# Ten attention weights of a hybrid decoder layer: their two parts made on GpSimd instead of ScalarE and VectorE

## The chip, the cores and the metric

The kernel runs on one core of a Trainium2 chip. A core has five engines that run side by side, each with its own queue of instructions: TensorE (PE, matrix products; its weight loads appear as PEld), VectorE (DVE), ScalarE (ACT), GpSimd (POOL) and SyncE (SP, which here issues DMAs). They pass data through SBUF and, for TensorE's results, PSUM. The metric is device time in microseconds (us) for one execution; less is better.

## The reference

One inference step of one layer on a prompt of 4096 tokens and 8 single-token samples, model width 1024, fp32:

- RMSNorm, then one projection by `w_in` into RG-LRU input (512), RG-LRU gate (512), queries (512), keys (128), values (128) and attention gate (512).
- Recurrence: a causal convolution of width 4, two block-diagonal gates r and i, h_t = a_t h_(t-1) + sqrt(1 - a_t^2) (i_t x_t) with a_t = sigmoid(L)^(8 r_t), times SiLU of its gate.
- Attention: 8 query heads on 2 key heads of 64, a sliding window of 128 keys, a relative-position bias, a sink per head, softmax; times SiLU of its gate.
- Both groups side by side, output projection by `w_out`, RMSNorm, residual. The states of convolution, recurrence and key/value window are outputs too.

## The kernel before

The 4096 tokens go in chunks: the first of 256 tokens with the 8 samples (264 columns), then ten of 384. Part A runs over all chunks: it normalizes and transposes x, projects it for the recurrence (`pr`), convolves, makes the gates (`gt`) and scans (line 352). It leaves the transposed x and its results in DRAM (`xT_d`, `mix_d`, line 362). Part B runs over all chunks again for attention: value, key, query and gate projections (`pv`, `pk`, `pq`, `pga`), then units of scores `S`, softmax, transposed probabilities `pT` and their product with the values `po`. Part C is the output projection.

Every fp32 product is split into three: a weight `ws` is turned into a rounded part `wh` and a rest `wl = ws - wh`, x into `xh` and `xl`, and `mm3` sums wh.xh + wh.xl + wl.xh. A projection of 128 output columns is thus 8 x 3 products. `load_w` makes the parts: the DMA to the staging tile `ws` (line 105, two buffers), the cast to `wh` by ACT (line 111), and the subtraction for `wl` by the engine `eng` (line 112), DVE unless told otherwise. Part A's first two weights already have their subtraction on GpSimd, after a cast on DVE (line 109).

The ten weights of part B are loaded in one loop (lines 754 to 757), in the order V, Q0, K, Q1, Q2, Q3, G0, G1, G2, G3 (G is the attention gate). The first eight take the eight slots of part A's weights, each as soon as part A's last product with the old weight is done; the last two lie in a pool `pb_late`, whose memory belongs to part A's last steps until these end. The loads of x for part B are issued by SP too (line 499).

The order of the instructions on each engine is not that of the code: a scheduler simulates the program with costs of its own and sets each engine's order when the kernel is built. An engine then works through its queue strictly in that order, and an instruction whose input or buffer isn't ready holds up all behind it. PE's projections in part B alternate between two PSUM banks: the products of Q2 can start when ACT and DVE have read K's bank, those of G0 when the copies and subtractions that make `sq` of Q2 (lines 567 to 570) have read Q2's.

The lines that matter around the hand-over from A to B: `thr`, `thi` (333, 334), `tt` (337), `aa`, `uu` (340, 341), the square root `uu` on ACT (348), the multiplications (350) and scans (352) of part A's last chunk; `kt` (487, 489), `ksT` (534), `sq` (567 to 570), masks (622), the minima `nm` (625), `ph` and `pl` (642, 643) of part B's first chunk.

Of the kernel before, what the change touches and what calls it, by code (L numbers as in the profile page):

```python
# [44 lines left out]
def hymba_kernel(ctx: ExitStack, tc: tile.TileContext, ins, outs):  # L45
    nc = tc.nc
# [56 lines left out]
    def load_w(src, n, pool, bufs=None, spare=None, eng=nc.vector, fast=False):  # L103
        ws = (spare or stage).tile([P, KD, P], F32, tag="ws", name=f"ws_{n}")
        nc.sync.dma_start(ws, src)
        wh = pool.tile([P, KD, P], F32R, tag="wh", name=f"wh_{n}", bufs=bufs)
        wl = pool.tile([P, KD, P], F32R, tag="wl", name=f"wl_{n}", bufs=bufs)
        if fast:
            nc.vector.tensor_copy(wh, ws)
        else:  # L110
            act(wh, ws, AF.Copy)
        eng.tensor_sub(wl, ws, wh)
        return wh, wl

    def load_w_in(m, pool=None, bufs=None, spare=None, eng=nc.vector, fast=False):
        return load_w(w_in_v[:, :, m * P:(m + 1) * P], f"in{m}", pool or wpool, bufs, spare, eng, fast)

    def load_w_out(e):
        return load_w(w_out_v[:, e, :].rearrange("p (k c) -> p k c", c=P), f"out{e}", wpool)
# [296 lines left out]
    wB = {}  # L416
# [335 lines left out]
    pbl, pb, pb1 = [c.__enter__() for c in cms]  # L752
    xB = load_x(0)
    for item in B_FIRST:
        if item[0] in "KVQG":
            m = {"K": 12, "V": 13, "Q": 8, "G": 14}[item[0]] + (int(item[1]) if item[0] in "QG" else 0)
            wB[m] = load_w_in(m) if len(wB) < 8 else load_w_in(m, pbl, 2)
    state = [{} for _ in chunks]
    state[0]["xs"] = xB
    work = [chunk_B(ci, state[ci], state[ci - 1]) for ci in range(NCH)]  # L760
# [121 lines left out]
def build(nc, arrays):  # L882
    args = []
    for name in _INS + ['onehot']:
        a = arrays[f"in_{name}_dram"]
        args.append(nc.dram_tensor(f"in_{name}_dram", a.shape, mybir.dt.from_np(a.dtype), kind="ExternalInput").ap())
    res = []
    for i, (shape, dtype) in enumerate(_OUTS):
        res.append(nc.dram_tensor(f"out_{i}_dram", shape, F32, kind="ExternalOutput").ap())
    with tile.TileContext(nc, schedule_with_timeline_sim=True) as tc:  # L890
        hymba_kernel(tc, args, res)
# [13 lines left out]
```

## Time and profile before

| | us |
|---|---|
| median of 3 runs | 1445.58 (1444.28 to 1446.62) |
| the profiled execution | 1449.84 |
| its span, first to last instruction | 1448.1 |
| PE busy | 1403.7 (97%) |
| DVE busy | 915.0 (63%) |
| ACT busy | 799.9 (55%) |
| POOL busy | 440.8 (30%) |

The profile is of one execution. Busy time counts an engine's own instructions; PE at 97% says that over the whole span there are some 44 us in which it had nothing to do. The tables by stretches say where those are, and the granted clock (1.00 is the full 2.4 GHz) how fast PE was allowed to run there. A wait row names the instruction that waited and the one on another engine that released it.

### The profile page before, as it was taken

What the parts mean: (1) busy time and instruction counts of PE and PEld (TensorE: products, weight loads), DVE (VectorE), ACT (ScalarE), POOL (GpSimd) and SP (SyncE); (2) the same over time, 40 slices, a digit from 0 to 9 for tenths busy, and PEclk for the clock granted to TensorE, in tenths of its full rate; (3) what the DMA queues carried; (4) which work ended last, traced back from release to release, by engine and by line L of the source; (5) the groups of instructions that cost most, each with busy time, mean ns of one, the idle gap of its engine ahead of it and who ended that gap; (6) DMA issues with size and microseconds to landing.
All of it is one profiled execution on the core that took longest, in us unless ns stands there. A gap on an engine that the chain in (4) does not pass through costs nothing.

```text
span 1448.1 us, 24120 instructions
## 1 busy us (share of the span) xinstructions
PE 1403.7 (97%) x8127; PEld 1324.1 (91%) x8127; DVE 915.0 (63%) x2258; ACT 799.9 (55%) x2055; POOL 440.8 (30%) x876
## 2 busy tenths in 40 slices
PE   5999999999999889999999999999999999999998
PEld 4999989999999789999999999999998888888886
DVE  6778877777778767657566566566784445334433
ACT  4656656755655656567676676576783222222211
POOL 3233332222421023364463453453543000000000
PEclk9999999999999989999999999999999999999999
DMA  8324454433236330320320320330444534443431
GB/s 269 134 85 153 148 169 143 148 136 129 98 127 192 99 117 25 122 100 13 109 99 12 110 99 12 110 99 12 162 134 148 165 136 141 146 132 133 147 128 60
DMA packets 115028, 170.23 MB, mean 118 GB/s; under 512 B 12214, under 2 KB 98822, under 8 KB 114906
## 3 DMA queue, kind: packets, MB, share of 16 engines
q1 hardware_dynamic: 114906, 168.71, 34.8%
q8 instruction: 64, 1.05, 0.3%
q14 instruction: 58, 0.48, 0.1%
HBM read 100.19 MB, written 68.50 MB: 116 GB/s over the span
## 4 chain that ended last, share of the span: by engine, by line
PE 68%; DVE 3%; ACT 2%; DMA 1%; issue 1%; SPq 0%; POOLq 0%; DVEq 0%; ACTq 0%
PE out L822 8%; PE out L824 8%; PE out L823 8%; PE pga L122 4%; PE pga L123 4%; PE pga L124 4%; PE pq L123 4%; PE pq L122 4%; PE pq L124 4%; PE po L664 3%; PE pT L638 2%; PE S L604 2%; PE S L605 2%; PE pr L122 1%; PE pr L123 1%; PE pr L124 1%
## 5 line engine op out<-in xcount | busy, mean ns | idle before, releaser
L123 PE MATMUL pr<-xl,wh_in 128*128 128x384 f32 (+1 forms) x688 | 231.9, 338 | 0.0
L122 PE MATMUL pr<-xh,wh_in 128*128 128x384 f32 (+1 forms) x688 | 220.1, 340 | 10.1 <-ACT xc L302 10.1
L124 PE MATMUL pr<-xh,wl_in 128*128 128x384 f32 (+1 forms) x688 | 229.8, 336 | 0.0
L822 PE MATMUL out<-wh_out,xh_mix_d 128*128 128x512 f32 (+1 forms) x520 | 201.2, 387 | 0.0
L823 PE MATMUL out<-wl_out,xh_mix_d 128*128 128x512 f32 (+1 forms) x520 | 200.9, 386 | 0.0
L824 PE MATMUL out<-wh_out,xl_mix_d 128*128 128x512 f32 (+1 forms) x520 | 200.5, 386 | 0.0
L841 ACT ACTIVATE sqc<-out 128x512 bf16<-128x512 f32 (+2 forms) x67 | 39.2, 585 | 192.5 <-PE out L824 182.4
L122 PEld LDWEIGHTS pr<-xh,wh_in 128*128 128x128 f32 x688 | 129.9, 191 | 11.9 <-ACT xc L302 11.6
L630 ACT ACTIVATE tt<-tt,nm 128x129 f32<-128x129 f32 x256 | 100.0, 393 | 71.9 <-DVE nm L627 71.7
L844 DVE TENSOR_TENSOR out<-out,gpost 128x512 f32<-128x512 f32 (+1 forms) x65 | 45.4, 699 | 148.0 <-ACT sqc L841 147.3
L123 PEld LDWEIGHTS pr<-xl,wh_in 128*128 128x128 f32 x688 | 131.3, 191 | 0.7 <-issue 0.7
L124 PEld LDWEIGHTS pr<-xh,wl_in 128*128 128x128 f32 x688 | 131.3, 191 | 0.0
L123 PE MATMUL pga<-xl_B,wh_in 128*128 128x384 f32 (+1 forms) x352 | 119.7, 340 | 0.0
L122 PE MATMUL pga<-xh_B,wh_in 128*128 128x384 f32 (+1 forms) x352 | 118.9, 338 | 0.7 <-ACT qz L574 0.7
L122 PE MATMUL pq<-xh_B,wh_in 128*128 128x384 f32 (+1 forms) x352 | 117.0, 333 | 1.3 <-DVE ksT L534 0.7
L124 PE MATMUL pga<-xh_B,wl_in 128*128 128x384 f32 (+1 forms) x352 | 118.0, 335 | 0.0
L123 PE MATMUL pq<-xl_B,wh_in 128*128 128x384 f32 (+1 forms) x352 | 117.3, 333 | 0.0
L124 PE MATMUL pq<-xh_B,wl_in 128*128 128x384 f32 (+1 forms) x352 | 117.1, 333 | 0.0
L141 POOL TENSOR_TENSOR rs_c<-ssc,mhalf 128x1 f32<-128x1 f32 (+1 forms) x33 | 20.5, 622 | 314.9 <-DVE ssc L845 286.2
L822 PEld LDWEIGHTS out<-wh_out,xh_mix_d 128*128 128x128 f32 x520 | 97.7, 188 | 19.9 <-issue 0.2
L824 PEld LDWEIGHTS out<-wh_out,xl_mix_d 128*128 128x128 f32 x520 | 97.7, 188 | 19.7
L823 PEld LDWEIGHTS out<-wl_out,xh_mix_d 128*128 128x128 f32 x520 | 97.7, 188 | 19.3
(258 smaller groups left out, 3565.0 us busy)
## 6 DMA issues: line engine op xcount, KB each, us to landing
xs<-in_x_prompt_dram SPq DMA_DIRECT2D x32, 512.0 KB
xr<-in_x_prompt_dram SPq DMA_DIRECT2D x32, 512.0 KB
out_dram<-xr SPq DMA_DIRECT2D x31, 512.0 KB
xT_d<-xh SPq DMA_DIRECT2D x80, 192.0 KB
xT_d<-xl SPq DMA_DIRECT2D x80, 192.0 KB
xf_mix_d<-mix_d SPq DMA_DIRECT2D x80, 192.0 KB
xh_B<-xT_d SPq DMA_DIRECT2D x80, 192.0 KB
xl_B<-xT_d SPq DMA_DIRECT2D x80, 192.0 KB
```

The costliest lines, as they stand in the source:

```text
L122: nc.tensor.matmul(out, wh, xh, start=first, stop=False)
L123: nc.tensor.matmul(out, wh, xl, start=False, stop=False)
L124: nc.tensor.matmul(out, wl, xh, start=False, stop=last)
L604: nc.tensor.matmul(o, qa, kt[:, kv, 0, kr], start=True, stop=False)
L605: nc.tensor.matmul(o, qa, kt[:, kv, 1, kr], start=False, stop=True)
L630: act(tt[:, g, 0:P + 1], tt[:, g, 0:P + 1], AF.Exp, scale=-1.0, bias=nm[:, g:g + 1], accum_out=sm[:, g:g + 1])
L664: nc.tensor.matmul(pog[:, :, r], v.rearrange("p l d -> p (l d)"), w[:, :, r], start=i == 0, stop=i == 2)
L822: nc.tensor.matmul(p, a, wh, start=st, stop=False)
L823: nc.tensor.matmul(p, a, wl, start=False, stop=False)
L824: nc.tensor.matmul(p, b, wh, start=False, stop=sp)
L841: act(sq[:rows, :c[1] - c[0]], p[:rows], AF.Square, scale=1.0 / 32.0, accum_out=ss[:rows, i:i + 1])
L844: nc.vector.tensor_mul(po[i][:rows], p[:rows], gpost[:rows, c[0]:c[1]])
```

## The change

In `load_w`, where `eng` is GpSimd (and `fast` isn't set), the cast to `wh` goes to GpSimd as well; and the loop over part B's ten weights passes `eng=nc.gpsimd`. Part A's first two weights use `fast` and keep their cast on DVE. Lines behind the first hunk have numbers higher by two in the changed kernel.

```diff
--- before.py
+++ after.py
@@ -107,6 +107,8 @@
         wl = pool.tile([P, KD, P], F32R, tag="wl", name=f"wl_{n}", bufs=bufs)
         if fast:
             nc.vector.tensor_copy(wh, ws)
+        elif eng is nc.gpsimd:
+            eng.tensor_copy(wh, ws)
         else:
             act(wh, ws, AF.Copy)
         eng.tensor_sub(wl, ws, wh)
@@ -754,7 +756,7 @@
     for item in B_FIRST:
         if item[0] in "KVQG":
             m = {"K": 12, "V": 13, "Q": 8, "G": 14}[item[0]] + (int(item[1]) if item[0] in "QG" else 0)
-            wB[m] = load_w_in(m) if len(wB) < 8 else load_w_in(m, pbl, 2)
+            wB[m] = load_w_in(m, eng=nc.gpsimd) if len(wB) < 8 else load_w_in(m, pbl, 2, eng=nc.gpsimd)
     state = [{} for _ in chunks]
     state[0]["xs"] = xB
     work = [chunk_B(ci, state[ci], state[ci - 1]) for ci in range(NCH)]
```

The scheduler makes a new order from this, in the hand-over alone. POOL, at the end of part A (`hl` is the scan's last column kept for the next chunk, `tt` the sink's column in the softmax, `xh` the convolution's three old columns). Before:

```order
L300 COPY xh_2_5406<-xr_2_5403 128x3
L295 COPY xr_3_5509<-xh_3_5078 128x3
L300 COPY xh_3_5512<-xr_3_5509 128x3
L615 COPY tt_0_0_5855<-bneg 128x4
L615 COPY tt_0_1_5905<-bneg 128x4
L615 COPY tt_1_0_6056<-bneg 128x4
L355 COPY hl_0_5568<-hh_0_5566 128x1
L355 COPY hl_1_5575<-hh_1_5573 128x1
L355 COPY hl_2_5582<-hh_2_5580 128x1
L355 COPY hl_3_5589<-hh_3_5587 128x1
L615 COPY tt_1_1_6135<-bneg 128x4
```

After, from the copy of `xh_3` on:

```order
L302 COPY xh_3_5512<-xr_3_5509 128x3
L111 CAST wh_in_5675<-ws_in_5673 128x1024
L111 CAST wh_in_5681<-ws_in_5679 128x1024
L114 TENSOR_TENSOR wl_in_5676<-ws_in_5673,wh_in_5675 128x1024
L617 COPY tt_0_0_5855<-bneg 128x4
L617 COPY tt_0_1_5905<-bneg 128x4
L617 COPY tt_1_0_6056<-bneg 128x4
L114 TENSOR_TENSOR wl_in_5682<-ws_in_5679,wh_in_5681 128x1024
L111 CAST wh_in_5687<-ws_in_5685 128x1024
L357 COPY hl_0_5568<-hh_0_5566 128x1
L357 COPY hl_1_5575<-hh_1_5573 128x1
L357 COPY hl_2_5582<-hh_2_5580 128x1
```

The casts and subtractions of the weights stand between the small copies; each subtraction of `wl` has another weight's cast ahead of it. DVE, where the last chunk of part A ends and the first scores are masked. Before:

```order
L341 SCALAR_TENSOR_TENSOR uu_5420<-thr_3_5552 128x384
L534 COPY ksT<-pk_5779 128x8
L622 COPY_PREDICATED S_0_0_5846<-msk,big 128x4x128
L569 TENSOR_TENSOR sq_2_5977<-pq_2_5952,sq_2_5977 64x256
L570 TENSOR_TENSOR sq_2_5977<-pq_2_5952,sq_2_5977 64x256
L557 SCALAR_TENSOR_TENSOR vs_0_5740<-pvt_5737,vs_0_5740 128x2x64
L527 COPY kt_6339<-kt_5778 128x4x128
L622 COPY_PREDICATED S_0_1_5889<-msk,S_0_1_5889 128x4x128
L625 ISA tt_0_0_5855,nm_0_0_5858<-S_0_0_5846,bneg 128x128
```

After:

```order
L352 TENSOR_TENSOR thi_2_5534<-thi_2_5534,uu_5420 128x384
L352 TENSOR_TENSOR thi_3_5553<-thi_3_5553,uu_5420 128x384
L559 SCALAR_TENSOR_TENSOR vs_1_5741<-pvt_5737,vs_1_5741 128x2x64
L354 SCALAR_TENSOR_TENSOR hh_0_5566<-aa_0_5452,hl_0_5261,thi_0_5448 128x384
L354 SCALAR_TENSOR_TENSOR hh_1_5573<-aa_1_5433,hl_1_5268,thi_1_5429 128x384
L354 SCALAR_TENSOR_TENSOR hh_2_5580<-aa_2_5538,hl_2_5275,thi_2_5534 128x384
L354 SCALAR_TENSOR_TENSOR hh_3_5587<-aa_3_5557,hl_3_5282,thi_3_5553 128x384
L624 COPY_PREDICATED S_0_0_5846<-msk,big 128x4x128
L624 COPY_PREDICATED S_0_1_5889<-msk,S_0_1_5889 128x4x128
L571 TENSOR_TENSOR sq_2_5977<-pq_2_5952,sq_2_5977 64x256
L572 TENSOR_TENSOR sq_2_5977<-pq_2_5952,sq_2_5977 64x256
```

The multiplications (now line 352) and the scans (now line 354) of the last chunk stand ahead of the two masks and of the subtractions `sq_2`; before, they came behind these and behind the first minima. SP, where the weights five to eight (`ws_in_5673` to `ws_in_5691`) are issued; `xh_B` and `xl_B` with a number from 6244 on are the x of chunk one. Before:

```order
L105 DMA ws_in_5679<-in_w_in_dram 128x8x128
L499 DMA xh_B_0_6244<-xT_d_79 128x384
L499 DMA xl_B_0_6246<-xT_d_79 128x384
L499 DMA xh_B_1_6248<-xT_d_79 128x384
L499 DMA xl_B_1_6250<-xT_d_79 128x384
L499 DMA xh_B_2_6252<-xT_d_79 128x384
L105 DMA ws_in_5685<-in_w_in_dram 128x8x128
L499 DMA xl_B_2_6254<-xT_d_79 128x384
L499 DMA xh_B_3_6256<-xT_d_79 128x384
L499 DMA xl_B_3_6258<-xT_d_79 128x384
L105 DMA ws_in_5691<-in_w_in_dram 128x8x128
L105 DMA ws_in_5697<-in_w_in_dram 128x8x128
```

After:

```order
L501 DMA xh_B_1_6248<-xT_d_79 128x384
L501 DMA xl_B_1_6250<-xT_d_79 128x384
L501 DMA xh_B_2_6252<-xT_d_79 128x384
L501 DMA xl_B_2_6254<-xT_d_79 128x384
L501 DMA xh_B_3_6256<-xT_d_79 128x384
L501 DMA xl_B_3_6258<-xT_d_79 128x384
L105 DMA ws_in_5673<-in_w_in_dram 128x8x128
L105 DMA ws_in_5679<-in_w_in_dram 128x8x128
L105 DMA ws_in_5685<-in_w_in_dram 128x8x128
L105 DMA ws_in_5691<-in_w_in_dram 128x8x128
L364 DMA mix_d_99<-hh_0_5566 128x384
L364 DMA mix_d_99<-hh_1_5573 128x384
```

All eight loads of x for chunk one (the first two stand just ahead of these rows) now come ahead of the fifth weight, and the last two weights' issues moved behind the four stores `mix_d_99`. On PE, before, the first products of `pv` and `pq` are strewn among the last `pr` of part A:

```order
L123 MATMUL pr_0_2_5287<-xl_7_5185,wh_in_301 128x384
L124 MATMUL pr_0_2_5287<-xh_7_5184,wl_in_302 128x384
L122 MATMUL pv_5709<-xh_B_0_5617,wh_in_5651 128x264
L123 MATMUL pv_5709<-xl_B_0_5619,wh_in_5651 128x264
L122 MATMUL pr_2_1_5353<-xh_0_4990,wh_in_307 128x384
L123 MATMUL pr_2_1_5353<-xl_0_4991,wh_in_307 128x384
```

After, part A's `pr` are all done when V begins:

```order
L124 MATMUL pr_3_2_5460<-xh_7_5184,wh_in_325 128x384
L125 MATMUL pr_3_2_5460<-xl_7_5185,wh_in_325 128x384
L126 MATMUL pr_3_2_5460<-xh_7_5184,wl_in_326 128x384
L124 MATMUL pv_5709<-xh_B_0_5617,wh_in_5651 128x264
L125 MATMUL pv_5709<-xl_B_0_5619,wh_in_5651 128x264
L126 MATMUL pv_5709<-xh_B_0_5617,wl_in_5652 128x264
```

From there PE's queue reads `pv`, `gt_2`, `pq_0`, `pk` with `gt_3` inside, `pq_1`, first scores, `pq_2`, scores, `pq_3`, two products of `pga_0`, the scores of the second head pair, `pga_0` and `pga_1`.

## Rows read from the trace of the kernel before

**Rows 1.** The page, section 2: busy tenths of TensorE in 40 slices

```profile
PE   5999999999999889999999999999999999999998
```

**Rows 2.** Stretches: busy us (count) of PE, PEld, DVE, ACT, POOL; clock, DMA, GB/s

```profile
460.00:480.00 20.00, 18.97 (x129) 18.76 (x127) 14.96 (x26) 9.42 (x16) 1.55 (x2) 1.00 0.92 284
480.00:500.00 20.00, 16.44 (x114) 15.66 (x115) 17.26 (x45) 16.01 (x33) 0.88 (x3) 0.91 0.18 54
500.00:520.00 20.00, 12.88 (x73) 11.49 (x72) 17.77 (x55) 12.29 (x41) 2.74 (x6) 0.80 0.11 41
520.00:540.00 20.00, 20.00 (x127) 19.86 (x127) 9.70 (x21) 10.93 (x32) 9.48 (x21) 0.94 0.52 172
```

**Rows 3.** Waits of PE, 447 to 540 us: total, times, longest

```profile
PE po L647 <- ACT ph L642: 3.5, 1, 3.5
PE gt L122 <- ACT thi L334: 3.0, 1, 3.0
PE po L647 <- DVE pl L643: 1.0, 1, 1.0
```

**Rows 4.** Timeline of ACT: start, us, what [idle before it, releaser]

```profile
476.79 1.06 ACT L111 ACTIVATE wh_in<-ws_in 128x1024 fp32r<-128x1024 f32 x1 [1.55 <-DMA ws_in<-in_w_in_dram]
...
494.70 1.28 ACT L348 ACT_TABLE_LOAD   x1
496.00 1.49 ACT L348 ACTIVATE uu<-uu 128x1536 f32<-128x1536 f32 x1
...
512.51 2.00 ACT L111 ACTIVATE wh_in<-ws_in 128x1024 fp32r<-128x1024 f32 x2 [3.70 <-DMA mix_d<-hh]
514.54 0.60 ACT L642 ACTIVATE ph<-pT 128x512 fp32r<-128x512 f32 x1
```

**Rows 5.** Line 111, casts of weights: ns min/median/max, first and last start

```profile
L111 ACT ACTIVATE wh_in<-ws_in x16: 1040/1060/1062, 11.7 to 513.5; 128x1024 fp32r<-128x1024 f32 x16
```

**Rows 6.** Line 112, subtractions, the same columns

```profile
L112 DVE TENSOR_TENSOR wl_in<-ws_in,wh_in x16: 1200/1219/1227, 14.7 to 514.8; 128x1024 fp32r<-128x1024 f32 x16
...
L112 POOL TENSOR_TENSOR wl_in<-ws_in,wh_in x2: 2345/3149/3953, 10.6 to 14.2; 128x1024 fp32r<-128x1024 f32 x2
```

**Rows 7.** Line 166 (scaling of x by its norm), the same columns

```profile
L166 POOL TENSOR_SCALAR xs<-xs,rs x30: 1121/1416/2675, 20.0 to 415.5; 128x1024 f32<-128x1024 f32 x30
```

**Rows 8.** PE by line, 451.3 to 501: xcount, busy, mean ns, idle

```profile
L123 PE MATMUL pr<-xl,wh_in 128*128 128x384 f32 x33 | 11.0, 335 | 0.0
```

**Rows 9.** Timeline of PE

```profile
451.46 0.28 PE L123 MATMUL pv<-xl_B,wh_in 128*128 128x264 f32 x1
451.58 0.34 PE L122 MATMUL pr<-xh,wh_in 128*128 128x384 f32 x1
...
455.58 0.33 PE L124 MATMUL pr<-xh,wl_in 128*128 128x384 f32 x1
```

**Rows 10.** Timeline of DVE

```profile
495.46 0.74 DVE L622 COPY_PREDICATED_SCALAR S<-msk,big 128x512 f32 x1
496.24 0.42 DVE L569 TENSOR_TENSOR sq<-pq,sq 64x256 fp32r<-64x256 f32 x1
...
499.11 1.96 DVE L350 TENSOR_TENSOR thi<-thi,uu 128x384 f32<-128x384 f32 x4
...
504.17 2.83 DVE L352 TENSOR_TENSOR_SCAN hh<-aa,hl,thi 128x384 f32<-128x384 f32 x3
```

**Rows 11.** Timeline of all engines from 204 us

```profile
204.27 0.53 DVE L318 SCALAR_TENSOR_TENSOR sg<-thg,pr 128x384 f32<-128x384 f32 x1
...
204.56 1.12 POOL L166 TENSOR_SCALAR xs<-xs,rs 128x1024 f32<-128x1024 f32 x1
...
204.72 1.38 DVE L361 TENSOR_TENSOR hh<-hh,sg 128x384 f32<-128x384 f32 x1
```

**Rows 12.** Timeline of DVE early in the kernel

```profile
16.97 2.26 DVE L428 TENSOR_TENSOR gwl<-gwf,gwh 128x1024 fp32r<-128x1024 f32 x1 [0.26 <-ACT gwh L427]
```

**Rows 13.** Timeline of the Sync queue (SPq): DMA issues

```profile
470.21 0.38 SPq L105 DMA_DIRECT2D ws_in<-in_w_in_dram  x1
```

## The prediction

> **What bounds the kernel now.** I read the page first. Its row of TensorE (PE) by slices is at nine tenths and above except at the start and in slices 14 and 15, about 470 to 543 us [rows 1]. That is the hand-over from part A (recurrence) to part B (attention), the only place where the order of the changed program differs. After it PE has no gap, so what the hand-over gains or loses is carried to the end one for one. Next the table by stretches: from 460 to 520 us PE is idle for 1.0, 3.6 and 7.1 us, 11.7 in all, and its granted clock falls to 0.91, 0.80 and 0.94 [rows 2]. What the lower clock costs is busy time times the missing share: 16.4 x 0.09 + 12.9 x 0.20 + 20.0 x 0.06 = 5.3 us. Third the waits of PE [rows 3]. The gate matmul `gt` waits 3.0 for `thi` on ScalarE (ACT): ACT stands at line 111 until a weight's DMA has landed (cast at 476.79), and the last gates' activations come late behind such casts. The matmul `po` waits 3.5 for `ph` on ACT, which stood for 3.7 us before the casts of weights nine and ten; they take 2.00, and only then comes `ph` [rows 4]. And `po` waits 1.0 more for `pl` on VectorE (DVE), which sits behind those weights' subtractions. So waits and clock cost 11.7 + 5.3 = 17.0 us, and 7.5 of the waits go back to the ten weights.
>
> **The change part by part.** *Removed:* ten casts on ACT, 1.06 us each, 10.6 us, and ten subtractions on DVE, 1.22 each, 12.2 us [rows 5, 6]. ACT and DVE are not the bound, so this is worth only the waits that stood behind them. The 3.0 goes: `thi` then follows its gate at once. Of the 4.5 at `po` I leave 1.7: `ph` (0.6) and `pl` (about the same) still follow the transposes [rows 4], with a fraction for the hand-over. Gain 5.8.
>
> *Added on GpSimd (POOL):* ten casts and ten subtractions of 128x1024. The subtraction has two rows on POOL, 2.35 and 3.95 [rows 6]. The cast has none; its bounds are a one-input scaling of the same size, 1.12 to 2.68, median 1.42 [rows 7]. I take the near ends, 1.1 and 2.3, since POOL's work around it is small; that is 3.4 per weight and 34 us in all, beside stretches that last 80. In sentences of its own: the Trainium skill (GPSIMD Engine Reference, section 3.1) gives 4497 ns for a two-input fp32 operation with twice the columns, so an estimate of 2.25 us for ours; the 2.35 row agrees, the 3.95 row does not, and by it the third rival below would fall away. Section 4.1 there puts elementwise work on VectorE, GpSimd being about twice as slow with two inputs; 2.35 against 1.22 agrees.
>
> *Moved:* the scheduler reorders the hand-over. PE first ends all of part A, then come V, gate 2, Q0, K with gate 3, Q1, Q2, Q3, then G0. From 451.3 the trace has 98 products `pr` up to 501 (33 + 33 + 32 by line) [rows 8], two of them begun before, so 96, and the gates 0 and 1 have six each: 108. A product of 384 columns takes 0.174 (24 of them from 451.58 to 455.58, 23 steps), one of 264 columns 0.12 (451.46 to 451.58) [rows 9]. Part A ends at 451.3 + 18.8 = 470.1. A projection of 264 columns is 24 x 0.12 = 2.9, a gate 6 x 0.174 = 1.0. V, gate 2, Q0, K, gate 3, Q1 end at 470.1 + 4 x 2.9 + 2 x 1.0 = 483.7; transposes and first scores 1.1, Q2 2.9, scores 0.9, Q3 2.9 bring PE to G0 at 491.5 (both small terms are estimates: nine and eight products of 128 columns at the 0.12 of 264). G0 needs the PSUM bank of Q2, which DVE's two subtractions `sq` free. These now stand behind the last chunk's four multiplications and four scans and two masks, which before came after or were spread. The chain: Q1 ends at 483.7; ACT's two copies of it, 0.4 each by DVE's 0.42 for the like, the table load 1.28 and the square root 1.49 [rows 4] bring 487.3; on DVE the multiplications take 1.96, the scans 4 x 0.94 = 3.8, two masks of 0.74, `sq` 2 x 0.42 [rows 10]: 495.4. G0 waits 3.9. The scores of the second pair then wait for DVE once more, for a release that stands behind the first unit's minima and `sq` of Q3; I put 1.9 (half of G0's wait). These two are new, 5.8, and take back the 5.8 that was gained.
>
> What stands of small waits (11.7 - 7.5 = 4.2) either stays, or is halved as ACT and DVE have less to do. Clock loss goes with idle time, 5.3 / 11.7 = 0.45 us for each. So without anything else the change is worth between 0 and -2.1 x 1.45 = -3.0; I take **-2**, nearer the second, since no cast is left between ACT's copies.
>
> *The shared port.* DVE's product with two SBUF inputs took 1.38 while POOL ran a 1.12 us scaling; one of the same size that reads PSUM, begun just before, took 0.53 [rows 11]. Early in the kernel, beside POOL's subtraction of 3.95 us (from 14.2), a DVE subtraction took 2.26 where its like takes 1.22 [rows 12, 6]. So an operation of DVE that meets one of POOL loses about 0.8 (1.38 less 0.55) with a cast and at least 1.04 with a subtraction. In sentences apart: the Trainium skill (GPSIMD Engine Reference, section 8, Key points) says that GpSimd shares its SBUF interfaces with VectorE and contends with DVE instructions that have two SBUF inputs. The pair 1.38 and 0.53 agrees, and this is the page's word against the change. Sixteen such operations (eight weights) fall before 505 us: if each met DVE on the path it is 8 x 0.8 + 8 x 1.04 = 14.7 us, if none, 0. Those of weights one to four come while PE has part A and V queued up, which covers them; the eight of weights five to eight fall in 477 to 499, where the chain to G0 runs, and DVE was busy 17.3 of 20 us there [rows 2], of which I leave it 0.8. 8 x 0.8 x 0.92 = 5.9, **+6**.
>
> *Sync queue.* Weights five to eight are now issued behind all loads of x for chunk one, which wait for PE's last product of part A (470.1, eight issues of some 0.4, so 473). Before, the one issued at 470.21 was cast at 476.79 [rows 4, 13]; the fifth now lands at 477 to 479, and two casts and a subtraction end 4.5 later, at 482 to 484, just ahead of Q2 at 484.8. It costs nothing, with no reserve; what it costs without cover is in the third rival. The last two weights wait on POOL behind four stores, with masks of `p` behind them; PE has G1 to G3 and chunk one's Q to do by then: nothing.
>
> Sum: -2 + 6 = **+4**. The profiled execution took 1449.84, 1.7 more than its span, so 1453.8 on its scale; it lies 4.26 above the median of the runs shown, on whose scale this is 1445.58 + 4 = **1449.5** (rounded).
>
> **Rivals.** *1, POOL's holds miss the chain* (the other side): the waits at line 111 go, and DVE meets POOL only where PE is covered: -2 to -3, **1443**. For it: the K and Q copies read PSUM, and such an operation was not slowed. Against it: multiplications, scans and gate arithmetic have two SBUF inputs. It turns at about two holds on the chain (2 / 0.92). *2, it cancels:* two or three holds; waits change places, the sum is within 1.5: **1446**. For it: gains and new waits of 5.8 each. *3, POOL itself late:* it pays 2.68 and 3.95, as where DVE is busy. Weight five is then ready at 478 + 2 x 2.68 + 3.95 = 487.3, 2.5 late; weight seven is staged only after that (about 4 us), and is ready at 491.3 + 2 x 2.68 + 3.95 = 500.6, 9 past G0's 491.5, where 3.9 were counted: 5 more, and half of it again by the clock. With the 4 of the forecast, some +12: **1458**. For it the 3.95 row; against it 2.35, and the median scaling of 1.42. That the ten weights stay where they were is no case: the changed order has them on POOL.
>
> **How the numbers follow.** Forecast +4 (own range +1.5 to +7, 1447 to 1452.5) 0.50; rival 1 0.17, rival 2 0.18, rival 3 0.15. About 0.2%, 2.9 us, is what a measurement of this kernel can tell from no change. Slower by more: 0.7 of the forecast's 0.50 and all of rival 3, 0.50; faster by more: 0.75 of rival 1, 0.13; the rest 0.37. The range 1443.5 to 1455.5 leaves out the lower part of rival 1 and most of rival 3, under 0.2.
>
> **What would show it.** Right: PE's waits on `thi` (3.0) and `ph` (3.5) are gone; a new wait of `pga` on DVE's `sq`, 4 us or more, stands near 490; DVE's gate arithmetic and scans between 477 and 499 have rows of 1.1 to 2 us where they took 0.55 or 0.94, beside POOL's rows at lines 111 and 114; the clock stays under 1 as long as before. Wrong: POOL's casts well over 1.2 us or subtractions over 2.6, with PE waiting for `wh` or `wl` (rival 3); DVE rows of normal length and PE's waits below 10 us (rival 1). If the difference arises outside 440 to 560, the whole argument fails.

## The result: 10.7 us slower, and the profile after

The changed kernel takes 1455.95 us (median of 6 runs, 1452.86 to 1458.92) against 1445.26 for the kernel before (6 runs, 1444.02 to 1447.69): a ratio of 1.0072, interval 1.0054 to 1.0090, which is 7.8 to 13.0 us. The direction is the predicted one; the size is 2.7 times the forecast of +4, and lies just above the range. The profiled run of the changed kernel took 1458.92 with a span of 1456.8, so it is 9.1 longer than that of before.

In the row of TensorE (PE) by slices of the changed kernel's page the loss lies where the prediction looked. Slice 14 falls from 8 tenths [rows 1] to 7, and all others stay:

```profile
PE   5999999999999789999999999999999999999998
```

The stretches of the changed kernel (columns as in [rows 2]: busy time of PE, PEld, VectorE (DVE), ScalarE (ACT), GpSimd (POOL), then clock, DMA share, GB/s):

```profile
460.00:480.00 20.00, 17.20 (x111) 16.58 (x112) 19.25 (x32) 9.42 (x18) 9.52 (x8) 1.00 0.84 259
480.00:500.00 20.00, 16.00 (x114) 15.34 (x112) 16.87 (x31) 9.96 (x22) 12.59 (x12) 0.91 0.26 72
500.00:520.00 20.00, 12.17 (x69) 11.32 (x69) 14.43 (x54) 11.33 (x43) 10.47 (x8) 0.74 0.31 93
520.00:540.00 20.00, 16.96 (x90) 15.34 (x90) 9.19 (x18) 7.16 (x23) 7.94 (x14) 0.75 0.30 87
```

From 460 to 540 PE is idle for 2.8 + 4.0 + 7.8 + 3.0 = 17.6 us, where it was 11.7. The lower clock costs 16.0 x 0.09 + 12.2 x 0.26 + 17.0 x 0.25 = 8.9, where it was 5.3. Together 26.5 against 17.0: 9.5 more, beside the 9.1 by which the two profiled runs differ. So nothing has to be looked for elsewhere. DVE is busy 19.25 of 20 us from 460 to 480, where it was 14.96 [rows 2], although the subtractions of the weights are gone from it.

PE's waits from 440 to 570, the changed kernel (total, times, longest):

```profile
PE pga L124 <- ACT qz L576: 3.7, 1, 3.7
PE S L606 <- DVE nm L627: 3.5, 1, 3.5
PE gt L124 <- DVE xk L314: 3.0, 2, 2.5
PE pq L124 <- ACT qz L576: 2.1, 1, 2.1
PE po L649 <- ACT ph L644: 1.8, 1, 1.8
PE pT L640 <- DVE pl L645: 1.1, 1, 1.1
PE pq L124 <- DVE sgb L587: 0.9, 1, 0.9
PE pq L125 <- DMA xl_B<-xT_d: 0.9, 1, 0.9
PE pq L124 <- DVE ksT L536: 0.7, 1, 0.7
```

Against [rows 3]: the 3.0 on `thi` is gone, and 1.7 of the 3.5 on `ph`. In their place stand four waits, of which the prediction had two. `pga` begins at 502.50, after ACT's `qz`, two copies of 0.37 us together that themselves wait for DVE's `sq`, as this row of the changed kernel's timeline shows (ACT):

```profile
502.03 0.37 ACT L576 ACTIVATE qz<-pq 64x8 f32<-64x8 f32 x2 [2.40 <-DVE sq L572]
```

Why DVE is late is seen when its timeline is laid beside POOL's. First POOL, the changed kernel:

```profile
446.90 2.70 POOL L111 CAST wh_in<-ws_in 128x1024 fp32r<-128x1024 f32 x2 [14.17 <-PE pr L125]
...
451.93 3.10 POOL L114 TENSOR_TENSOR wl_in<-ws_in,wh_in 128x1024 fp32r<-128x1024 f32 x1
...
457.27 2.78 POOL L114 TENSOR_TENSOR wl_in<-ws_in,wh_in 128x1024 fp32r<-128x1024 f32 x1
...
471.89 5.36 POOL L114 TENSOR_TENSOR wl_in<-ws_in,wh_in 128x1024 fp32r<-128x1024 f32 x2
...
480.74 2.88 POOL L111 CAST wh_in<-ws_in 128x1024 fp32r<-128x1024 f32 x2 [3.03 <-DMA ws_in<-in_w_in_dram]
483.59 2.66 POOL L114 TENSOR_TENSOR wl_in<-ws_in,wh_in 128x1024 fp32r<-128x1024 f32 x1
...
500.91 4.96 POOL L114 TENSOR_TENSOR wl_in<-ws_in,wh_in 128x1024 fp32r<-128x1024 f32 x2
```

and DVE, the same kernel (line 306 is the convolution's sum, 352 and 354 multiplications and scans, 363 the gated product that goes to DRAM as `mix_d`):

```profile
446.83 3.65 DVE L352 TENSOR_TENSOR thi<-thi,uu 128x384 f32<-128x384 f32 x4 [1.55 <-ACT uu L350]
...
453.21 3.54 DVE L354 TENSOR_TENSOR_SCAN hh<-aa,hl,thi 128x384 f32<-128x384 f32 x2
456.68 4.85 DVE L306 SCALAR_TENSOR_TENSOR xc<-xr,cT,xc 128x384 f32<-128x384 f32 x5
...
472.45 5.22 DVE L306 SCALAR_TENSOR_TENSOR xc<-xr,cT,xc 128x384 f32<-128x384 f32 x2
...
481.65 1.08 DVE L342 TENSOR_SCALAR aa<-thr 128x384 f32<-128x384 f32 x1
482.65 1.39 DVE L343 SCALAR_TENSOR_TENSOR uu<-thr 128x384 f32<-128x384 f32 x1
484.05 0.42 DVE L571 TENSOR_TENSOR sq<-pq,sq 64x256 fp32r<-64x256 f32 x1
...
502.88 3.42 DVE L363 TENSOR_TENSOR hh<-hh,sg 128x384 f32<-128x384 f32 x2
```

Read each long DVE row with the POOL row that covers its time. Two convolution sums of some 0.6 each take 5.22 while POOL subtracts twice for 5.36. The four multiplications took 1.96 before [rows 10] and take 3.65 beside two casts. The minima `nm`, for which `S` waits 3.5, stand behind the 3.42 at 502.88, most of which lies inside POOL's 4.96 from 500.91. The row of 0.42 at 484.05, which reads PSUM, keeps its length beside a subtraction of 2.66.

POOL's operations themselves (the changed kernel's lines 111 and 114 on POOL: ns min/median/max, first and last start) are little slower than [rows 6, 7] let one expect:

```profile
L111 POOL CAST wh_in<-ws_in x10: 1035/1336/1772, 446.9 to 515.5; 128x1024 fp32r<-128x1024 f32 x10
```

```profile
L114 POOL TENSOR_TENSOR wl_in<-ws_in,wh_in x12: 2332/2655/3947, 10.2 to 524.7; 128x1024 fp32r<-128x1024 f32 x12
```

and PE waits for a weight from POOL once, a weight load of Q2 for 0.9 us.

### The profile page after: what moved, and what is told of

Its sections match the earlier page's. It is cut to its first block, busy times and chain, and to the rows that moved or that the text cites. A ratio compares the mean times of both kernels' runs of the same rounds, so it can differ in the third digit from the quotient of the medians.

```text
span 1456.8 us, 24126 instructions
## 1 busy us (share of the span) xinstructions
PE 1407.0 (97%) x8127; PEld 1325.9 (91%) x8127; DVE 920.1 (63%) x2248; ACT 789.4 (54%) x2045; POOL 475.4 (33%) x896
## 4 chain that ended last, share of the span: by engine, by line
PE 69%; DVE 3%; ACT 2%; issue 1%; DMA 1%; POOLq 0%; DVEq 0%; ACTq 0%; SPq 0%
PE out L824 8%; PE out L826 8%; PE out L825 8%; PE pga L126 4%; PE pga L125 4%; PE pga L124 4%; PE pq L124 4%; PE pq L125 4%; PE pq L126 4%; PE po L666 3%; PE pT L640 2%; PE S L606 2%; PE S L607 2%; PE pr L124 2%; PE pr L125 1%; PE pr L126 1%
```

## The experiments

Two things change at once here: the engine that does the work, and, because the scheduler sees other engines, the order of every engine's queue in the hand-over. To tell them apart each kernel below is built twice. The first build has the engines of one of the two kernels (ORDER_OF) and gives the order; in the second (RUN) every engine's queue is held to that order by edges that carry no semaphore. So only the named instructions differ. The frame, common to all:

```diff
+RUN = ["PP"] * 10        # engines of cast and subtraction: A ScalarE, D VectorE, P GpSimd
+ORDER_OF = ["AD"] * 10   # "AD": the order of before, "PP": that of the changed kernel
...
+        prev = last.get(ins.engine)
+        if prev is not None:
+            tc.add_manual_dep(ins, prev.name, mybir.DependencyInfo(mybir.DependencyClass.NoSync,
+                              mybir.DependencyReason.DATA), reason="order")
+        last[ins.engine] = ins
```

In substance three theories stand against each other, with the names that the expectations use: that DVE is held by POOL at a shared port (PORT, the prediction's +6), that the new order costs the time (ORDER), and that POOL delivers late (LATE). Line numbers are larger in these kernels than in the two of the change; the names in a row tell what it is. All were timed in five rounds against the kernel before on the same chip. No run holds the kernel before to its own order with nothing else changed; e4, e12 and e14, which change two to four weights, lie within 1 us of it, so the holding itself costs nothing that shows.

| run | order of | POOL does | median us | before | ratio (interval) |
|---|---|---|---|---|---|
| e1_before_order | before | all ten | 1454.97 | 1446.47 | 1.0057 (1.0040 to 1.0074) |
| e2_after_order | after | none | 1456.17 | 1446.47 | 1.0075 (1.0057 to 1.0092) |
| e3_w1to4 | before | weights 1 to 4 | 1455.76 | 1446.47 | 1.0068 (1.0051 to 1.0085) |
| e4_w9to10 | before | weights 9, 10 | 1446.24 | 1446.47 | 0.9998 (0.9987 to 1.0008) |
| e5_after_small | after | all, an eighth of the columns | 1446.97 | 1446.38 | 1.0004 (0.9990 to 1.0017) |
| e6_before_small | before | all, an eighth of the columns | 1441.31 | 1446.38 | 0.9957 (0.9941 to 0.9974) |
| e7_after_pieces | after | all, in eight pieces each | 1453.59 | 1446.38 | 1.0043 (1.0030 to 1.0057) |
| e8_w5to8 | before | weights 5 to 8 | 1448.00 | 1446.38 | 1.0008 (0.9994 to 1.0022) |
| e9_after_w1to4 | after | 1 to 4 in full, six an eighth | 1452.52 | 1444.77 | 1.0048 (1.0029 to 1.0067) |
| e10_after_w5to8 | after | 5 to 8 in full, six an eighth | 1449.33 | 1444.77 | 1.0028 (1.0015 to 1.0042) |
| e11_after_late | after | an eighth, held back too long | 1460.79 | 1444.77 | 1.0102 (1.0082 to 1.0123) |
| e12_casts_back | before, two casts later | none | 1445.36 | 1444.77 | 0.9997 (0.9984 to 1.0009) |
| e13_after_late2 | after | an eighth, held back as after | 1446.72 | 1446.19 | 1.0013 (1.0002 to 1.0024) |
| e14_combo | before, two casts later | weights 9, 10 | 1445.30 | 1446.19 | 0.9996 (0.9983 to 1.0009) |

The runs of one kernel spread by 4 to 10 us, and so differences of medians and ratios can differ by 1 us; where that matters both are given.

**The whole change in the old order, and the new order without the change.**

```diff
 e1_before_order: RUN = ["PP"] * 10, ORDER_OF = ["AD"] * 10
 e2_after_order:  RUN = ["AD"] * 10, ORDER_OF = ["PP"] * 10
```

> All ten weights are made on GpSimd, but every engine keeps the order of the kernel before: only the casts and subtractions change engine. Theory PORT (VectorE stands still while GpSimd holds the shared SBUF access): it stays slower than before, +5 to +13 us, and the trace has rows of VectorE with two SBUF inputs of 1.1 us and more beside each GpSimd row of lines 111 and 114. Theory ORDER (the scheduler's new order, scans ahead of the copies of Q2, part A's products ahead of V, costs the time): within 2 us of before or faster, as the waits behind the ten casts on ScalarE are gone. Theory LATE (the weights are ready too late, 3.7 us each on GpSimd against 2.3): slower too, but with TensorE waiting for wh or wl, 5 us or more in all, and with VectorE's rows of normal length.

> The reverse: the casts are on ScalarE and the subtractions on VectorE as before, but every engine keeps the order of the changed kernel. PORT: the added time goes away, between -3 and +3 us to before. ORDER: it keeps +8 to +12 us, TensorE's wait of pga behind the scans stays at 3.7. LATE: the added time goes, as under PORT; only the first run tells the two apart.

Measured: +8.5 and +9.7. The first is what PORT expected, the second what ORDER did. Each half alone costs nearly as much as both together, so the two don't add, and these two runs name no culprit. The waits of e2, the new order with casts on ACT (total, times, longest), say more:

```profile
PE pga L130 <- ACT qz L582: 4.4, 1, 4.4
PE po L655 <- issue: 4.1, 1, 4.1
PE pq L130 <- ACT qz L582: 3.2, 1, 3.2
```

Two of them stand at the same products as in the changed kernel (3.7 and 2.1 there), but not because DVE is held: DVE's rows have their normal lengths in e2 (the four multiplications 1.97, two convolution sums 1.27). For `pq` ACT is late, which stood 3.86 for a weight's DMA before a cast at 475.03, with the copies `sq` and `qz` behind it. The wait of `pga` is that of the order itself, as e5 shows next.

**The same orders, with POOL's work cut to an eighth.** This takes away the length of POOL's operations, and keeps their number and places. These kernels leave out seven eighths of each weight; TensorE uses the one eighth eight times (`SMALL` lists such weights, `REAL` is set in the second build).

```diff
-            eng.tensor_copy(wh, ws)
+            c = 1 if REAL[0] else KD
+            nc.gpsimd.tensor_copy(wh[:, :c, :], ws[:, :c, :])
...
-            mm3(pm[:, :W], w[0][:, k, :], w[1][:, k, :], xs[0][k], xs[1][k], k == 0, k == KD - 1)
+            kw = 0 if any(w[0] is t for t in SMALL) else k
+            mm3(pm[:, :W], w[0][:, kw, :], w[1][:, kw, :], xs[0][k], xs[1][k], k == 0, k == KD - 1)
```

> Order of the changed kernel, casts and subtractions of the ten weights on GpSimd, but of one eighth of the columns (128 of 1024; TensorE uses that eighth for all eight parts of a weight, with as many products of the same size as before). So ScalarE and VectorE are rid of the work and GpSimd hardly holds the shared access. PORT: the added time goes; the prediction had -2 for this case, so between -5 and +2 us to before. ORDER: the new order costs by itself, it stays +6 to +11, with pga waiting 4 us behind the scans.

> The same with the order of the kernel before: what the removal from ScalarE and VectorE is worth by itself. The waits on thi (3.0) and ph (3.5) with their clock: -4 to -8 us to before. If these waits only change hands (transposes behind tt, keys behind VectorE): within 2 us.

Measured: +0.6 in the new order, -5.1 in the old one (by the ratio -6.2). This gives a decomposition of the +10.7, in the order in which the steps are taken: taking the work off ACT and DVE is worth -5.1, the new order then costs 5.7, and the full length of POOL's operations 10.1 (10.7 less the 0.6 of e5). In e5 the waits of PE are

```profile
PE pga L138 <- ACT qz L591: 3.7, 1, 3.7
PE po L664 <- ACT ph L659: 1.9, 1, 1.9
PE S L621 <- DVE nm L642: 1.6, 1, 1.6
```

with no wait of `gt` on `xk` and none of `pq` on `qz`, and `S` at 1.6 where the changed kernel has 3.5: these waits, 7.0 us, are what the length of POOL's operations adds. They are not the whole of it. The stretches of e5 with a lower clock (columns as above):

```profile
480.00:500.00 20.00, 14.02 (x100) 13.32 (x99) 17.18 (x49) 9.68 (x24) 4.01 (x9) 0.87 0.32 95
500.00:520.00 20.00, 16.07 (x102) 14.49 (x101) 10.63 (x38) 12.83 (x50) 6.30 (x16) 0.87 0.22 62
```

The lower clock costs 14.0 x 0.13 + 16.1 x 0.13 = 3.9 there, and 8.9 in the changed kernel. By this sum 5 us of the difference between these two profiled runs are clock.

**Which weights?** First in the old order, then in the new one:

```diff
 e3_w1to4:       RUN = ["PP"] * 4 + ["AD"] * 6,                ORDER_OF = ["AD"] * 10
 e8_w5to8:       RUN = ["AD"] * 4 + ["PP"] * 4 + ["AD"] * 2,   ORDER_OF = ["AD"] * 10
 e4_w9to10:      RUN = ["AD"] * 8 + ["PP"] * 2,                ORDER_OF = ["AD"] * 10
 e9_after_w1to4: RUN = ["PP"] * 4 + ["pp"] * 6,                ORDER_OF = ["PP"] * 10   # p: an eighth
 e10_after_w5to8: RUN = ["pp"] * 4 + ["PP"] * 4 + ["pp"] * 2,  ORDER_OF = ["PP"] * 10
```

> Order of the kernel before, only weights one to four (V, Q0, K, Q1) on GpSimd. The prediction held these to be covered by TensorE's queue of part A and V: 0 us, within 1.5. PORT with the stall that the changed kernel's trace shows (two convolution sums of VectorE took 5.22 us beside the subtractions of weights three and four): +3 to +6 us, with the gate matmul waiting for xk. ORDER and LATE: 0.

> Order of the kernel before, only weights five to eight (Q2, Q3, G0, G1) on GpSimd. The prediction put the whole cost of the shared access here, 6 us, against the gate's wait on thi of 3.0 that goes (4.4 with the clock): 0 to +3 us. By the run with weights one to four alone, which took +9.3, the cost sits there instead, and this is between -4 and +1.

> Order of the kernel before, only weights nine and ten (G2, G3) on GpSimd. Their casts stood on ScalarE ahead of ph. The prediction's gain: the wait of po on ph (3.5) and on pl (1.0) shrink to 1.7 together, -3 to -5 us with the clock. PORT: a little of it is lost where VectorE's products meet the two subtractions, -1 to -4 us. ORDER: -3 to -5. If ph is late for another reason (its transposes): 0.

> Order of the changed kernel, all ten weights on GpSimd, but only weights one to four with all 1024 columns; the other six with 128 (TensorE uses that eighth for all parts of them, with as many products as before). The run with all ten at 128 columns stood at +0.6 us to before, the changed kernel at +10.7, so 10 us lie between them. The prediction put 0 of it here (TensorE's queue covers the first four): 0 to +2. PORT by the traces (two convolution sums stood 5.2 us beside the subtractions of weights three and four): +5 to +9.

> The reverse: weights five to eight with all columns, the others with 128. The prediction put all of the shared access here: +6 to +8. If most sits at the first four weights: +2 to +5.

Measured in the old order: +9.3 for weights one to four alone, +1.6 for five to eight (not to be told from nothing), -0.2 for nine and ten. In the new one: +7.75 by medians (+6.9 by the ratio, interval +4.2 to +9.7) with one to four in full, +4.6 (+4.1, interval +2.2 to +6.1) with five to eight. Less the 0.6 of e5 that is 6.3 to 7.1 for the first four weights and 3.5 to 4.0 for the next four; with the 0.6 the sum is 10.4 to 11.7, beside the measured 10.7. That the first four cost a good deal is clear of these intervals; that they cost more than the next four is not, by the times alone.

How the first four reach PE is seen in e3. DVE, then POOL's two subtractions beside the last two of these rows:

```profile
445.64 5.84 DVE L358 TENSOR_TENSOR thi<-thi,uu 128x384 f32<-128x384 f32 x4 [1.55 <-ACT uu L356]
...
454.16 2.69 DVE L312 SCALAR_TENSOR_TENSOR xc<-xr,cT,xc 128x384 f32<-128x384 f32 x1
...
464.16 2.75 DVE L369 TENSOR_TENSOR hh<-hh,sg 128x384 f32<-128x384 f32 x1
```

```profile
453.27 3.15 POOL L120 TENSOR_TENSOR wl_in<-ws_in,wh_in 128x1024 fp32r<-128x1024 f32 x1
...
463.90 2.59 POOL L120 TENSOR_TENSOR wl_in<-ws_in,wh_in 128x1024 fp32r<-128x1024 f32 x1
```

the Sync queue (SP), in e3 and, in the last row, the same three stores in the kernel before:

```profile
460.27 6.98 SPq L370 DMA_DIRECT2D mix_d<-hh  x3
467.35 0.38 SPq L507 DMA_DIRECT2D xl_B<-xT_d  x1
```

```profile
459.27 1.79 SPq L362 DMA_DIRECT2D mix_d<-hh  x3
```

and PE's waits:

```profile
PE gt L130 <- ACT thi L342: 4.1, 1, 4.1
PE pv L130 <- DMA xh_B<-xT_d: 4.0, 2, 2.7
```

A multiplication, a convolution sum and a gated product, each held by POOL, make the products `hh` late; their three stores stand on SP for 6.98 us, where they took 1.79 before; behind them stand the loads of x for V, and PE waits 4.0 for these. The matmuls that were to cover DVE need loads that wait for DVE, and so the cover ran out. The wait on `xk` that had been expected did not come; the gate waits on `thi`, as before (3.0 there).

In e4 the last two weights are off ACT, and `ph` waits all the same, not behind a cast (timeline of ACT):

```profile
506.60 0.60 ACT L650 ACTIVATE ph<-pT 128x512 fp32r<-128x512 f32 x1 [3.69 <-DMA mix_d<-hh]
```

It is the same 3.7 before a `mix_d` store that the casts of nine and ten showed in [rows 4]. PE waits 1.4 and 1.1 at `po` instead of 3.5 and 1.0, but 2.2 on DVE's `tt` for `pT` (0.8 before), and the time stays. That wait for a DMA was not the casts' own.

**Held at the port, or late?** Cutting POOL's work to an eighth also makes it early. Two kernels put the lateness back without the long operations: tiny copies of one column are issued ahead of each small cast and subtraction (`later` keeps an instruction right behind the one issued before it).

```diff
+    def fill(count, src):
+        tiny = const.tile([P, 2], F32, name=f"tiny_{len(EXTRA)}")
+        nc.gpsimd.tensor_copy(tiny[:, 0:1], src[:, 0, 0:1].bitcast(F32))
+        for k in range(count - 1):
+            later(nc.gpsimd.tensor_copy(tiny[:, 1:2], tiny[:, 0:1]))
...
+            fill(7, ws)      # e13_after_late2: 4
+            later(nc.gpsimd.tensor_copy(wh[:, :c, :], ws[:, :c, :]))
...
+            fill(15, wh)     # e13_after_late2: 8
+            later(nc.gpsimd.tensor_sub(wl[:, :c, :], ws[:, :c, :], wh[:, :c, :]))
```

> Order of the changed kernel; each cast and subtraction on GpSimd with 128 columns, but behind 7 (cast) or 15 (subtraction) copies of one column, so that its result comes about as late as with 1024 columns (each such copy 0.15 us, estimated from three small copies of 0.44 us in a row), while no instruction holds the shared access for long. PORT: as with 128 columns alone, -2 to +4 us to before. LATE: as the changed kernel, +8 to +12, with TensorE waiting for the weights or for stores behind them.

> As the run with copies of one column ahead of each cast and subtraction, but 4 and 8 of them instead of 7 and 15: there a subtraction's group took 4 to 7 us on GpSimd, longer than the 2.65 us of the changed kernel, so it was later than meant. Now about 1.3 and 2.7 us (0.24 to 0.28 us for a copy). PORT: -1 to +4 us to before. LATE: +8 to +12. Waits of TensorE for wl that come with it say how much of the rest is lateness.

e11 overshot: +16, with groups of 4 to 7 us for what should have been one subtraction, and PE waiting for the weights themselves:

```profile
PE pq L156 <- POOL wl_in L138: 8.0, 1, 8.0
PE pga L156 <- POOL wl_in L138: 7.0, 3, 2.9
```

It shows only what real lateness would look like, and that the changed kernel, with 0.9, has next to none of it. e13 has the right length: a group of copies and its subtraction take 2.3 to 6.2 us in a row, as late as or later than the 2.3 to 3.1 that they stand for. It took +0.5 (by the ratio +1.9, interval +0.3 to +3.5), about what e5 took. Its longest wait of PE is 4.0 at `pga`, where e5 has 3.7. DVE in e13:

```profile
448.75 2.06 DVE L383 TENSOR_TENSOR thi<-thi,uu 128x384 f32<-128x384 f32 x4 [1.55 <-ACT uu L381]
...
453.57 1.91 DVE L385 TENSOR_TENSOR_SCAN hh<-aa,hl,thi 128x384 f32<-128x384 f32 x2
455.41 2.71 DVE L337 SCALAR_TENSOR_TENSOR xc<-xr,cT,xc 128x384 f32<-128x384 f32 x5
...
471.57 1.27 DVE L337 SCALAR_TENSOR_TENSOR xc<-xr,cT,xc 128x384 f32<-128x384 f32 x2 [0.46 <-ACT xc L335]
```

These are the same four groups, in the same order, that took 3.65, 3.54, 4.85 and 5.22 in the changed kernel. A busy and late POOL with short operations costs almost nothing; its long ones cost some 9 to 10 (10.7 less 0.5 to 1.9).

**Long operations cut in pieces.** The same work in eight instructions of 128 columns:

```diff
-            eng.tensor_copy(wh, ws)
+            for k in range(0, KD, c):
+                i = nc.gpsimd.tensor_copy(wh[:, k:k + c, :], ws[:, k:k + c, :])
...
-        eng.tensor_sub(wl, ws, wh)
+            for k in range(0, KD, c):
+                i = nc.gpsimd.tensor_sub(wl[:, k:k + c, :], ws[:, k:k + c, :], wh[:, k:k + c, :])
...
```

> Order of the changed kernel, each cast and subtraction on GpSimd cut into eight instructions of 128 columns. PORT, with access held for the length of one instruction: VectorE gets in between the pieces, its rows stay under 1 us, and the time falls to +1 to +6 of before, though GpSimd works some 10 us longer in all. If GpSimd keeps the access from piece to piece: +9 to +14. LATE: slower than the changed kernel, +11 to +16, as the weights are ready later still.

Measured: +7.2 (by the ratio +6.2), at or just above the upper end of what PORT expected, and 3.5 less than the changed kernel. DVE is nearly free again, and POOL is not; e7, all engines:

```profile
445.38 9.81 POOL L121 CAST wh_in<-ws_in 128x128 fp32r<-128x128 f32 x16 [14.17 <-PE pr L141]
...
452.20 2.84 DVE L322 SCALAR_TENSOR_TENSOR xc<-xr,cT,xc 128x384 f32<-128x384 f32 x5
```

Five sums take 2.84, not 4.85. But two casts take 9.81 where they took 2.70 (later ones 1.9 to 3.0 each), and PE now waits for x's loads (3.1), for `wl` (1.8) and for `hl` (1.3) from POOL. By these rows a DVE operation is held for up to the length of one POOL instruction, so pieces shorten the hold; what they add on POOL eats most of the gain.

**Is there anything to gain?** The wait on `thi` that the change removed can be had without POOL: the casts of weights seven and eight stand ten instructions later in ACT's queue.

```diff
+MOVES = [(6, 10, 0), (7, 10, 0)]   # (weight, instructions back: cast, subtraction), order of before
 e14_combo adds: RUN = ["AD"] * 8 + ["PP"] * 2
```

> The kernel before with its engines and order, but the casts of weights seven and eight (G0, G1) stand ten instructions later on ScalarE, behind the last gates' thr and thi; their subtractions follow them. The gate's wait of 3.0 on thi goes: with the clock -2 to -5 us to before. If a new wait takes its place (pga for the weights, pq for qz): within 1.5.

> A try at a better version: order of the kernel before, casts of weights seven and eight ten instructions later on ScalarE, weights nine and ten on GpSimd. Each alone made no difference. If the waits they remove only moved on to the next (xk, tt): within 1.5 us of before. If both together are needed to shorten the chain: -2 to -5.

Both took the time of the kernel before. The 3.0 on `thi` is gone in e12, and among PE's waits this stands in its place:

```profile
PE gt L137 <- DVE xk L327: 3.1, 1, 3.1
```

None of the fourteen beat the kernel before but e6, and that one makes an eighth of the weights: its -5.1 says what moving this work could bring in the old order if it cost POOL next to nothing. It is not a kernel to use.

## Why the prediction was right or wrong

**What bounds the kernel: right.** The difference arises in the hand-over alone, whose 9.5 us of idle time and lower clock account for the 9.1 between the profiled runs.

**Removed, gain 5.8: right as a sum of waits.** e6 keeps the old order and takes the work away: -5.1 (-6.2). Its profiled run has 6.1 us of idle time from 460 to 540, 5.6 less than before. That its time agrees too is in part luck: by the working's own price, 0.45 of clock for each us of idle time, 5.8 should have brought 8.4, but the clock loss fell by 1.0 alone (16.7 x 0.26 = 4.3, from 5.3). Nor was the step to the waits clean: e4 and e12 show that the wait on `ph` ends with a store, and that the 3.0 on `thi` turns into one on `xk` when only the cast is moved. The gain came only in e6, where DVE is rid of its subtractions too (`gt` waits 0.8 on `xk` there).

**Moved, 3.9 for `pga` and 1.9 for `S`: right.** e5 has 3.7 and 1.6, and its wait of `pga` ends at 493.89 where the working had 495.4. e6 against e5 puts the order at 5.7 by the times, the 5.8 of the working, and at 4.6 by the idle time. In the changed kernel the wait of `pga` ends at 502.50 and `S` waits 3.5, since subtractions on POOL hold the products ahead of the minima.

**Without the port -2: too good by 2.6.** e5 is at +0.6. The small waits were not halved: of the 4.2 there are 3.3 left in e5, 1.1, 0.9, 0.7 and 0.6, beside `po`'s 1.9.

**The Sync queue 0, weights nine and ten 0: right.** PE waits 0.9 for a weight; e4 is at -0.2. Weight five was ready at 486.25 and not at 482 to 484, but PE came to Q2 later too.

**The shared port, +6: here it failed.** The step is the sentence "Those of weights one to four come while PE has part A and V queued up, which covers them". They cost 6.3 to 7.1 us. PE's queue needs the gates, which need the convolution's sums from DVE (`gt` on `xk`, 3.0 in the changed kernel), and in the old order also x's loads, which stand on SP behind stores that need DVE (4.0 in e3, 4.2 in e1). The products that PE had queued did not cover the delay of DVE, 10.3 us by the rows below.

The term also carries no clock: the working charges 0.45 for each us of idle time in the term of -2 and in the third rival, and nothing here, while the changed kernel has 5 us more of clock loss than e5.

The price was also badly shared out. Against the same groups of e13, DVE loses beside the first four weights 1.6 + 1.6 + 2.1 + 4.0 (the four groups above), 0.65 at 466.26 and 0.4 at 471.42: 10.3 us. Four subtractions make up 7.7 of it, 1.9 each, where 1.04 was reckoned with; four casts 2.65, 0.66 each, where it was 0.8. Beside weights five to eight it loses 0.7 + 0.8 (481.65, 482.65), 0.6 (a row of 1.18 at 488.60, normally 0.56) and 2.4 at 502.88, 4.6 in all: half of POOL's operations meet rows that read PSUM, or nothing. That is 14.9 for sixteen, 0.93 each, which is the mean of the prediction's 0.8 and 1.04; but the eight that were written off as covered took twice what the other eight did. For these, 5.9 was predicted and 3.5 to 4.0 came, a gap that the spread of the runs could also make.

So the sum by measured terms is 0.6 + 6.3 to 7.1 + 3.5 to 4.0, and the forecast's was -2 + 0 + 6.

**The rivals.** The first (holds miss the chain, 1443) and the second (1446) fall by e5 against the changed kernel. The third named 1458, the closest time, for a wrong reason: POOL's casts were 1.34 and its subtractions 2.66 at the median, the weights were not waited for, and e13 shows that lateness of the measured size costs next to nothing. Of the signs that were named, `thi` gone and the long DVE rows beside lines 111 and 114 came, and the clock was under 1 from 480 to 540 as before, though lower (0.74 and 0.75 from 500 on). The wait of `pga` came with 3.7, but from 499 to 502 and not near 490; `ph` left 1.8; and most of the long rows stood before 477, where the prediction did not look.

**Open.** Why POOL's full length costs 13.6 in the old order (e1 less e6) and 10 in the new one is shown only in part, by the loads behind the stores in e3 and e1. Nor is it known whether an order made for this placement by other costs of the scheduler would keep the -5.

## What to carry to other kernels

When work goes to GpSimd, count every VectorE instruction with its operands in SBUF that will run beside it, at up to the length of the GpSimd instruction it meets (beside the first four weights here, in the mean, 0.66 of a cast's 1.34 us and 1.9 of a subtraction's 2.66), and follow each such delay through whatever queue reads its result, stores on the Sync queue too. "TensorE has work queued" covers a delay only if that work does not itself need the engine that is delayed. And a scheduler that reorders on such a change makes a second change: hold the order of one kernel and run the work of the other before putting a difference down to either.

## What was not expected of the hardware

- A VectorE row beside POOL's subtraction stood for up to the whole of it: 5.22 us for two sums of 0.6 beside 5.36 us of two subtractions. In eight pieces of 128 columns the same work lengthened five sums by 0.13 us in all (2.84 against 2.71), and other rows by up to 0.3 each.
- It is not only operations with two inputs in SBUF: `aa` (one input, 0.36) took 1.08 beside a cast. The Trainium skill (GPSIMD Engine Reference, section 8, Key points) names VectorE instructions with two SBUF inputs and those in a 2-port performance mode; the trace shows that this one-input instruction waits, but not in which mode it ran.
- POOL pays as well: a cast took 1.04 at best and 1.77 at worst, a subtraction of part B's weights 2.35 to 3.10 (part A's first two took 2.33 and 3.95, nearly as before [rows 6]). The cast of 1.77 and the subtraction of 3.10 ran where DVE was busy with operands in SBUF.
- Copies of one column cost 0.22 to 0.26 us each on POOL (three in 0.67, seven in 1.81), and up to 0.8 beside a busy DVE (seven in 5.56): short instructions are not free there.
